# Moving the splits, rotations and tables of a hybrid encoder block from GpSimd to VectorE

## The chip, the cores and the metric

The kernel runs on one core of a Trainium2 chip. A core has a matrix engine (TensorE, PE in the profile), a vector engine (VectorE, DVE), an engine for activation functions (ScalarE, ACT), a general-purpose engine (GpSimd, POOL) and a queue engine that issues the transfers (SyncE, SP). Each engine works through its own list of instructions in order and waits on semaphores for the others. The metric is the device time of one execution in microseconds (us); the time before is the median of three runs.

## The reference

One encoder block on a sequence of 1024 tokens of width 1024, all in float32:

```python
h = _rms_norm(x, norm_mix_g)
proj = h @ w_in            # gla q,k,v,r | gate codes fwd,bwd | swa q,k,v | gates a,b
y_gla = _gla_branch(...) @ w_o_gla     # 4 heads, chunked gated linear attention, both directions
y_swa = _swa_branch(...) @ w_o_swa     # 8 query heads on 2 key heads, window +-128, rotary, sinks
merged = sigmoid(gate_a) * y_gla + sigmoid(gate_b) * y_swa
x = x + merged @ w_out
h2 = _rms_norm(x, norm_ffn_g)
gu = h2 @ w_ffn_in
x = x + (silu(gu[..., :D_FF]) * gu[..., D_FF:]) @ w_ffn_out
```

In the window branch, queries and keys are normalised per head, multiplied by a gain and rotated by position (`x1*cos - x2*sin`, `x2*cos + x1*sin` on the two halves of 64).

## The kernel before, in words

**Products in three parts.** Matrix products run on float32r operands. To keep float32 accuracy each operand is split in two: a rounded high part `h` (a copy by ScalarE) and a low part `l = raw - h` (a subtraction). A product is then the sum of three matmuls, `h*h`, `h*l` and `l*h`. So every weight tile that is loaded gives one ScalarE copy and one subtraction, and so does every operand that the kernel makes itself. `wunit` (lines 62 to 69) does this for a weight tile of 128x512: transfer into `wr` (4 buffers), copy into `wh` (5 buffers), subtraction into `wl` (5 buffers). The subtraction (L68) is made by GpSimd, unless the caller gives another engine: `out_proj(1)` and the first feed-forward products `p11` and `p21` give VectorE.

**Stages in order of time.**

- Start, to about 50 us: the input is loaded in 16 tiles; `x_tile` makes `xh` (ScalarE, L263), `xl` (VectorE, L264) and the sums of squares (`acc`, L270). PE multiplies the first two weight columns as tiles arrive.
- Gated linear attention (GLA), to about 475 us: PE's order is written by hand. The work of 4 heads x 8 chunks goes through stages `g_gates`, `g_sums`, `g_scores`, `g_out`, `g_back_out` and `g_turn`, one slot apart, and between any two of them PE is given a number of dense matmuls of the input projection (`fill`, `slot`; 31 a slot in the middle). `next_unit` keeps the weight tiles of the dense work two units ahead of their use (`AHEAD = 2`). `g_sums` makes from the gates the scaled queries `q2` and keys `kh`, `kl` of a chunk (L360 to L368); `g_scores` splits the values `vh`, `vl` (L378, L379), transposes the keys and computes the scores (`sp`, split into `sh` and `sl` at L395 and L396); `g_out` uses them. GpSimd makes the low parts at L366, L368 and L379.
- Windowed attention, to about 775 us, filled in the same way with dense matmuls: GpSimd makes three of the four tables `qA`, `qB` (cosine and sine times the query gain, L513 to L516). `k_prep` loads the keys and values of a block, splits the values (`vSl`, L557) and normalises and rotates the keys (`norm_rope`, L523 to L543; two of its products on GpSimd at L537 and L538). `k_turn` transposes the rotated keys (L563). `a_prep` normalises and rotates the queries (two products on GpSimd, L577 and L579, the others on VectorE, L581 and L582), then `a_turn`, `a_scores`, `a_probs` and `a_out` follow, each a slot later.
- Branch products, to about 1050 us: `prep_a`, `prep_b` load and split the outputs of the two mixers; `branch_a`, `branch_b` and `out_proj` multiply them by three weight matrices in `hgroup`, two `wunit` tiles for each output tile.
- Feed-forward, the rest: sums and differences of weights on GpSimd and VectorE (`comb`, L848), splits in `wsplit` (VectorE, L830), gates on GpSimd (L878, L921, L937).

**The order.** PE's instructions run in the order of the program. For the other engines a planner puts the instructions in order when the kernel is built, by their place in the program and by when they could start in its own estimate. On the chip each engine keeps that order, so an instruction that waits holds up those behind it on its engine. All transfers are issued by SyncE.

Of the kernel before, what the change touches and what calls it, by code (L numbers as in the profile page):

```python
# [8 lines left out]
F32 = mybir.dt.float32  # L9
# [20 lines left out]
def body(tc, i, out):  # L30
    nc = tc.nc
    with ExitStack() as root:
# [26 lines left out]
            nc.sync.dma_start(out=t, in_=src)  # L59
            return t  # L60

        def wunit(src, n=512, e=None):
            raw = wp.tile([P, n], F32, tag="wr", name=nm("wr"), bufs=4)
            nc.sync.dma_start(out=raw, in_=src)
            h = wp.tile([P, n], FR, tag="wh", name=nm("wh"), bufs=5)
            nc.scalar.activation(h, raw, AF.Copy)  # L66
            l = wp.tile([P, n], FR, tag="wl", name=nm("wl"), bufs=5)
            (e or nc.gpsimd).tensor_tensor(l, raw, h.bitcast(F32), op=ALU.subtract)  # L68
            return h, l

        def mm(o, a, b, start, stop):
# [273 lines left out]
        def g_sums(hd, c):  # L345

            a = gla[hd, c]
            bp = chtile((P, 2, 256))
            for d in range(2):
                mm(bp[:, d], a.lh[:, d], U, True, False)  # L350
                mm(bp[:, d], a.ll[:, d], U, False, True)

            a.sm = gtile("sm", (P, 2, 2), bufs=32)
            nc.vector.tensor_copy(a.sm, bp[:, :, 127:129])
            bc = bp.rearrange("p a (c t) -> p (a c) t", c=2)[:, 0:4:3]
            eb = gtile("eb", (P, 2, P), bufs=1)
            a.en = gtile("en", (P, 2, P))
            nc.scalar.activation(eb, bc, AF.Exp)
            nc.scalar.activation(a.en, bc, AF.Exp, scale=-1.0)
            nc.vector.tensor_tensor(eb, eb, a.qk[:, 0:1].to_broadcast([P, 2, P]), op=ALU.mult)  # L360
            nc.vector.tensor_tensor(a.en, a.en, a.qk[:, 1:2].to_broadcast([P, 2, P]), op=ALU.mult)
            a.q2 = gtile(f"q2{c}", (P, 2, 2, P), FR, bufs=2 if c < 5 else 1)
            a.kh = gtile("kh", (P, 2, P), FR)
            a.kl = gtile("kl", (P, 2, P), FR)
            nc.scalar.activation(a.q2[:, :, 0], eb, AF.Copy)
            nc.gpsimd.tensor_tensor(a.q2[:, :, 1], eb, a.q2[:, :, 0].bitcast(F32), op=ALU.subtract)  # L366
            nc.scalar.activation(a.kh, a.en, AF.Copy)
            nc.gpsimd.tensor_tensor(a.kl, a.en, a.kh.bitcast(F32), op=ALU.subtract)  # L368

        def g_scores(hd, c):  # L370

            a = gla[hd, c]
            need((f"v{hd // 2}", c))
            vr = gtile("vr", bufs=1)
            nc.sync.dma_start(out=vr, in_=scr[f"v{hd // 2}", c][:, (hd % 2) * 256:(hd % 2) * 256 + 256])
            a.vh = gtile("vh", dt=FR)
            a.vl = gtile("vl", dt=FR)
            nc.scalar.activation(a.vh, vr, AF.Copy)  # L378
            nc.gpsimd.tensor_tensor(a.vl, vr, a.vh.bitcast(F32), op=ALU.subtract)  # L379
            kt = chtile((P, 2, P))  # L380
            for d in range(2):
                nc.tensor.transpose(kt[:, d], a.en[:, d], ident)
            a.kth = gtile("kth", (P, 2, P), FR)
            a.ktl = gtile("ktl", (P, 2, P), FR)
            nc.scalar.activation(a.kth, kt, AF.Copy)
            nc.vector.tensor_tensor(a.ktl, kt, a.kth.bitcast(F32), op=ALU.subtract)
            sc = chtile((P, 2, P))
            for d in range(2):
                mm3(sc[:, d], a.kh[:, d], a.kl[:, d], a.q2[:, d, 0], a.q2[:, d, 1], True, True)
            sp = gtile("sp", (P, P))  # L390
            nc.scalar.copy(sp, sc[:, 0])
            nc.vector.copy_predicated(sp, tri, sc[:, 1])
            a.sh = gtile("sh", (P, P), FR)
            a.sl = gtile("sl", (P, P), FR)
            nc.vector.tensor_copy(a.sh, sp)  # L395
            nc.vector.tensor_tensor(a.sl, sp, a.sh.bitcast(F32), op=ALU.subtract)  # L396
# [113 lines left out]
        qA = sc_.tile([P, KT, P], F32, tag="qA", name="qA")  # L510
        qB = sc_.tile([P, KT, P], F32, tag="qB", name="qB")
        gb_ = [qg[:, None, h * 64:(h + 1) * 64].to_broadcast([P, KT, 64]) for h in range(2)]
        nc.gpsimd.tensor_tensor(qA[:, :, 0:64], cosb, gb_[0], op=ALU.mult)  # L513
        nc.gpsimd.tensor_tensor(qA[:, :, 64:128], cosb, gb_[1], op=ALU.mult)
        nc.vector.scalar_tensor_tensor(qB[:, :, 0:64], sinb, -1.0, gb_[1], op0=ALU.mult, op1=ALU.mult)
        nc.gpsimd.tensor_tensor(qB[:, :, 64:128], sinb, gb_[0], op=ALU.mult)  # L516

        def inv_norm(raw, n, sq, scale, epsv, eps_t):
            ss = sw.tile([P, n], F32, tag=f"ss{n}", name=nm("ss"))
# [6 lines left out]
        def norm_rope(raw, n, t, gain, scale, epsv, eps_t):  # L526

            sq = sw.tile([P, n, P], F32, tag=f"sq{n}", name=nm("sq"))
            rs = inv_norm(raw, n, sq, scale, epsv, eps_t)
            qn = sw.tile([P, n, P], F32, tag=f"qn{n}", name=nm("qn"))  # L530
            for h in range(n):
                nc.vector.scalar_tensor_tensor(qn[:, h], raw[:, h], rs[:, h:h + 1], gain,
                                               op0=ALU.mult, op1=ALU.mult)
            c = cosb[:, t:t + 1].to_broadcast([P, n, 64])
            s = sinb[:, t:t + 1].to_broadcast([P, n, 64])
            b = sq
            nc.gpsimd.tensor_tensor(b[:, :, 0:64], qn[:, :, 64:128], s, op=ALU.mult)  # L537
            nc.gpsimd.tensor_tensor(b[:, :, 64:128], qn[:, :, 0:64], s, op=ALU.mult)  # L538
            nc.vector.tensor_tensor(qn[:, :, 0:64], qn[:, :, 0:64], c, op=ALU.mult)
            nc.vector.tensor_tensor(qn[:, :, 64:128], qn[:, :, 64:128], c, op=ALU.mult)  # L540
            nc.vector.tensor_tensor(qn[:, :, 0:64], qn[:, :, 0:64], b[:, :, 0:64], op=ALU.subtract)
            nc.vector.tensor_tensor(qn[:, :, 64:128], qn[:, :, 64:128], b[:, :, 64:128], op=ALU.add)
            return qn  # L543
# [7 lines left out]
        def k_prep(t):  # L551
            kv = sw.tile([P, 4, P], F32, tag="kvr", name=nm("kvr"), bufs=1)
            need(("skv", t))
            nc.sync.dma_start(out=kv.rearrange("p a b -> p (a b)"), in_=scr["skv", t])
            v2 = kv[:, 2:4].rearrange("p a b -> p (a b)")
            nc.scalar.activation(vSh[t], v2, AF.Copy)
            nc.gpsimd.tensor_tensor(vSl[t], v2, vSh[t].bitcast(F32), op=ALU.subtract)  # L557
            keys[t] = norm_rope(kv[:, 0:2], 2, t, kg, 1.0 / 128, EPS, epst)

        def k_turn(t):  # L560
# [7 lines left out]
        def a_prep(g, n):  # L568
            a = att[g, n] = Chunk()
            need((f"sq{g}", n))  # L570
            qr = sw.tile([P, 4, P], F32, tag="qr", name=nm("qr"))
            nc.sync.dma_start(out=qr.rearrange("p a b -> p (a b)"), in_=scr[f"sq{g}", n])

            b = sw.tile([P, 4, P], F32, tag="sq4", name=nm("sq"))
            a.rs = inv_norm(qr, 4, b, 1.0, EPS * 128, eps128)
            a.qn = sw.tile([P, 4, P], F32, tag="qn4", name=nm("qn"))
            nc.gpsimd.tensor_tensor(b[:, :, 0:64], qr[:, :, 64:128], qB[:, n:n + 1, 0:64].to_broadcast([P, 4, 64]),  # L577
                                    op=ALU.mult)
            nc.gpsimd.tensor_tensor(b[:, :, 64:128], qr[:, :, 0:64], qB[:, n:n + 1, 64:128].to_broadcast([P, 4, 64]),  # L579
                                    op=ALU.mult)  # L580
            nc.vector.tensor_tensor(a.qn, qr, qA[:, n:n + 1].to_broadcast([P, 4, P]), op=ALU.mult)  # L581
            nc.vector.tensor_tensor(a.qn, a.qn, b, op=ALU.add)  # L582
# [133 lines left out]
        def btile(tag, dt=F32, bufs=None):  # L716
            return bt.tile([P, HT], dt, tag=tag, name=nm(tag), bufs=bufs)

        def hgroup(w, u0, ah, al, e=None):
            b = mmtile()  # L720
            for u in range(2):
                h, l = wunit(w[u0, u], e=e)
                for kk in range(4):
                    k = u * 4 + kk
                    c = slice(kk * P, (kk + 1) * P)
                    mm3(b, h[:, c], l[:, c], ah[k], al[k], k == 0, k == KT - 1)
            return b
# [58 lines left out]
        def out_proj(s):  # L786
            a = acc[:, s * HT:(s + 1) * HT]
            for j, m in enumerate((0, 4, 1, 5, 2, 6, 3, 7)):
                xr = fi.tile([P, HT], F32, tag="lx", name=nm("lx"), bufs=2)
                nc.sync.dma_start(out=xr, in_=i["xT"][m, s])  # L790
                y = hgroup(i["w_out"], m, mh, ml, nc.vector if s else None)
                nc.vector.tensor_tensor(xr, y, xr, op=ALU.add)
                d = scratch(f"x1_{m}_{s}")
                nc.sync.dma_start(out=d, in_=xr)
# [97 lines left out]
        def p11(f):  # L892
            F = feats[f]
            F.Y = mmtile()
            if f < NB:
                w = wunit(i["w_fi"][f, 0], e=nc.vector)
            else:
                F.r11 = rload(f, 11)
                w = wsplit(F.r11, 512)
# [3 lines left out]

        def p21(f):
            F = feats[f]
            w = wunit(i["w_fi"][f, 1], e=nc.vector) if f < NB else wsplit(F.r12, 512)
            product(F.Y, w, YX["21"], 4, False, True)
            F.g0 = gate0(F.Y, "a" if f < NA else "g0")

# [264 lines left out]
```

## Time and profile before

| | before |
|---|---|
| median of 3 runs (lowest to highest) | 1748.46 us (1748.05 to 1749.23) |
| profiled execution, its own time | 1748.99 us |
| its span, first to last instruction | 1747.2 us |
| TensorE (PE) busy | 1701.6 us, 97% |
| VectorE (DVE) busy, instructions | 1105.4 us, 63%, 1998 |
| ScalarE (ACT) busy | 866.4 us, 50% |
| GpSimd (POOL) busy, instructions | 564.4 us, 32%, 491 |
| mean granted clock of TensorE | 0.993 |

Busy means that an instruction of the engine is in progress; a matmul's end is modelled, and a few records can be missing. In lists of instructions a line gives the start, the length, the engine, the source line, the operation, output and inputs by the program's names, their sizes, and in square brackets how long the engine had idled before it and what ended that. In groups, the count is followed by busy time, mean length in ns, and the idle time before its members. A waiting row says who waited, for whom, for how long in total, how often, and the longest.

### The profile page before, as it was taken

How to read it: one execution, taken by the hardware profiler on the slowest of the kernel's cores; microseconds unless marked ns; L12 is line 12 of the kernel's file. 1: busy time of each engine (PE TensorE's matmuls, PEld its weight loads, DVE VectorE, ACT ScalarE, POOL GpSimd, SP SyncE). 2: the span in 40 equal slices, each digit the busy share in tenths (PEclk: the TensorE clock that was granted, in tenths of full speed). 3: DMA queues.
4: the chain of work that ended last, by engine and by line, in shares of the span. 5: the costliest groups of instructions: out<-in, count | busy, mean ns of one | idle time of the engine just before them, and what ended most of it. 6: DMA issues, size and time to landing. Idle time of an engine off the chain costs nothing. (4 is left out here: it accounts for less than half of the span.)

```text
span 1747.2 us, 24463 instructions
## 1 busy us (share of the span) xinstructions
PE 1701.6 (97%) x8008; PEld 1408.8 (81%) x8008; DVE 1105.4 (63%) x1998; ACT 866.4 (50%) x2019; POOL 564.4 (32%) x491
## 2 busy tenths in 40 slices
PE   8999999999999999999999999999999999899998
PEld 6788888888778888878878888788888888787776
DVE  6446666664387655536463268877788888789454
ACT  6455766776447656544454456533333333343342
POOL 3444535544353222112455430333343333100000
PEclk9999999999999999999999999999999999999999
DMA  5433343444533232227766645333234434685333
GB/s 193 138 113 103 119 129 120 122 129 138 167 118 118 88 97 91 79 73 246 238 192 187 193 132 181 109 132 127 91 102 146 152 138 140 233 295 170 96 96 103
DMA packets 158496, 246.03 MB, mean 141 GB/s; under 512 B 18111, under 2 KB 47807, under 8 KB 158369
## 3 DMA queue, kind: packets, MB, share of 16 engines
q1 hardware_dynamic: 158368, 244.48, 43.8%
q8 instruction: 63, 1.03, 0.3%
q14 instruction: 65, 0.52, 0.1%
HBM read 177.30 MB, written 67.11 MB: 140 GB/s over the span
## 5 line engine op out<-in xcount | busy, mean ns | idle before, releaser
L68 POOL TENSOR_TENSOR wl<-wr,wh 128x512 fp32r<-128x512 f32 (+1 forms) x226 | 300.3, 1334 | 471.3 <-ACT wh L66 395.3
L66 ACT ACTIVATE wh<-wr 128x512 fp32r<-128x512 f32 (+1 forms) x256 | 158.1, 625 | 133.7 <-PE mm L72 89.6
L72 PE MATMUL mm<-xh,wh 128*128 128x512 f32 x512 | 205.4, 401 | 6.7 <-ACT xh L263 6.7
L72 PE MATMUL mm<-xl,wh 128*128 128x512 f32 x512 | 205.1, 401 | 0.9 <-DVE xl L264 0.9
L72 PE MATMUL mm<-xh,wl 128*128 128x512 f32 x512 | 172.2, 401 | 0.0
L848 POOL TENSOR_TENSOR ws<-wr,wr 128x512 f32<-128x512 f32 x44 | 67.0, 1525 | 231.3 <-DMA wr<-in_w_fi_dram 126.3
L72 PE MATMUL mm<-wh,xh 128*128 128x512 f32 x320 | 127.0, 397 | 2.6 <-ACT st L210 1.3
L72 PE MATMUL mm<-wh,xl 128*128 128x512 f32 x320 | 126.8, 396 | 0.0
L72 PE MATMUL mm<-wl,xh 128*128 128x512 f32 x320 | 126.3, 395 | 0.0
L72 PEld LDWEIGHTS mm<-xh,wh 128*128 128x128 f32 x512 | 98.0, 191 | 23.3 <-ACT xh L263 6.7
L72 PEld LDWEIGHTS mm<-xl,wh 128*128 128x128 f32 x512 | 97.9, 191 | 18.7 <-DVE xl L264 1.9
L72 PEld LDWEIGHTS mm<-xh,wl 128*128 128x128 f32 x512 | 96.0, 191 | 16.7
L829 ACT ACTIVATE wh<-ws 128x512 fp32r<-128x512 f32 x88 | 55.4, 629 | 98.7 <-PE ch L856 41.5
L829 ACT ACTIVATE wh<-a 128x512 fp32r<-128x512 f32 x66 | 41.7, 632 | 103.2 <-PE mm L992 58.0
L830 DVE TENSOR_TENSOR wl<-ws,wh 128x512 fp32r<-128x512 f32 x88 | 76.4, 875 | 13.5 <-ACT wh L829 13.5
L992 PE MATMUL mm<-hl,wh 128*128 128x512 f32 x176 | 70.7, 402 | 11.0 <-DVE hl L967 11.0
L830 DVE TENSOR_TENSOR wl<-a,wh 128x512 fp32r<-128x512 f32 x66 | 45.5, 691 | 55.1 <-ACT wh L829 55.0
L829 ACT ACTIVATE wh<-wr 128x512 fp32r<-128x512 f32 x52 | 32.9, 632 | 77.9 <-PE ch L856 39.3
L72 PEld LDWEIGHTS mm<-wh,xh 128*128 128x128 f32 x320 | 60.3, 188 | 13.9 <-ACT st L210 2.0
L992 PE MATMUL mm<-hh,wh 128*128 128x512 f32 x176 | 70.0, 398 | 1.2 <-ACT hh L966 1.2
L992 PE MATMUL mm<-hh,wl 128*128 128x512 f32 x176 | 70.1, 398 | 0.0
L72 PEld LDWEIGHTS mm<-wh,xl 128*128 128x128 f32 x320 | 60.3, 188 | 10.0
(502 smaller groups left out, 4785.9 us busy)
## 6 DMA issues: line engine op xcount, KB each, us to landing
wr<-in_w_fi_dram SPq DMA_DIRECT2D x102, 256.0 KB, 2.8
wr<-in_w_t_dram SPq DMA_DIRECT2D x80, 256.0 KB, 2.7
wr<-in_w_f_dram SPq DMA_DIRECT2D x64, 256.0 KB, 2.8
B<-c SPq DMA_DIRECT2D x44, 256.0 KB, 2.1
T<-tx SPq DMA_DIRECT2D x44, 256.0 KB, 2.2
a<-in_w_fo_dram SPq DMA_DIRECT2D x44, 256.0 KB, 4.9
hr<-T SPq DMA_DIRECT2D x44, 256.0 KB, 2.7
hr<-B SPq DMA_DIRECT2D x33, 256.0 KB, 4.0
```

The lines of the kernel that those rows point to most:

```text
L66: nc.scalar.activation(h, raw, AF.Copy)
L68: (e or nc.gpsimd).tensor_tensor(l, raw, h.bitcast(F32), op=ALU.subtract)
L72: nc.tensor.matmul(o, a, b, start=start, stop=stop)
L829: nc.scalar.activation(h, src, AF.Copy)
L830: nc.vector.tensor_tensor(l, src, h.bitcast(F32), op=ALU.subtract)
L848: e.tensor_tensor(t, x, y, op=op)
L992: nc.tensor.matmul(ys[m], a[:, c], b, start=f0, stop=f1, skip_group_check=True)
```

## The change

All of GpSimd's work ahead of the feed-forward part becomes VectorE's. Nothing else differs: the same instructions on the same tiles, in the same places of the program. GpSimd keeps its weight sums and gates of the feed-forward part.

```diff
-        def wunit(src, n=512, e=None):
+        def wunit(src, n=512):
...
-            (e or nc.gpsimd).tensor_tensor(l, raw, h.bitcast(F32), op=ALU.subtract)
+            nc.vector.tensor_tensor(l, raw, h.bitcast(F32), op=ALU.subtract)
...
-            nc.gpsimd.tensor_tensor(a.q2[:, :, 1], eb, a.q2[:, :, 0].bitcast(F32), op=ALU.subtract)
+            nc.vector.tensor_tensor(a.q2[:, :, 1], eb, a.q2[:, :, 0].bitcast(F32), op=ALU.subtract)
...
-            nc.gpsimd.tensor_tensor(a.kl, a.en, a.kh.bitcast(F32), op=ALU.subtract)
+            nc.vector.tensor_tensor(a.kl, a.en, a.kh.bitcast(F32), op=ALU.subtract)
...
-            nc.gpsimd.tensor_tensor(a.vl, vr, a.vh.bitcast(F32), op=ALU.subtract)
+            nc.vector.tensor_tensor(a.vl, vr, a.vh.bitcast(F32), op=ALU.subtract)
...
-        nc.gpsimd.tensor_tensor(qA[:, :, 0:64], cosb, gb_[0], op=ALU.mult)
-        nc.gpsimd.tensor_tensor(qA[:, :, 64:128], cosb, gb_[1], op=ALU.mult)
+        nc.vector.tensor_tensor(qA[:, :, 0:64], cosb, gb_[0], op=ALU.mult)
+        nc.vector.tensor_tensor(qA[:, :, 64:128], cosb, gb_[1], op=ALU.mult)
...
-        nc.gpsimd.tensor_tensor(qB[:, :, 64:128], sinb, gb_[0], op=ALU.mult)
+        nc.vector.tensor_tensor(qB[:, :, 64:128], sinb, gb_[0], op=ALU.mult)
...
-            nc.gpsimd.tensor_tensor(b[:, :, 0:64], qn[:, :, 64:128], s, op=ALU.mult)
-            nc.gpsimd.tensor_tensor(b[:, :, 64:128], qn[:, :, 0:64], s, op=ALU.mult)
+            nc.vector.tensor_tensor(b[:, :, 0:64], qn[:, :, 64:128], s, op=ALU.mult)
+            nc.vector.tensor_tensor(b[:, :, 64:128], qn[:, :, 0:64], s, op=ALU.mult)
...
-            nc.gpsimd.tensor_tensor(vSl[t], v2, vSh[t].bitcast(F32), op=ALU.subtract)
+            nc.vector.tensor_tensor(vSl[t], v2, vSh[t].bitcast(F32), op=ALU.subtract)
...
-            nc.gpsimd.tensor_tensor(b[:, :, 0:64], qr[:, :, 64:128], qB[:, n:n + 1, 0:64].to_broadcast([P, 4, 64]),
+            nc.vector.tensor_tensor(b[:, :, 0:64], qr[:, :, 64:128], qB[:, n:n + 1, 0:64].to_broadcast([P, 4, 64]),
...
-            nc.gpsimd.tensor_tensor(b[:, :, 64:128], qr[:, :, 0:64], qB[:, n:n + 1, 64:128].to_broadcast([P, 4, 64]),
+            nc.vector.tensor_tensor(b[:, :, 64:128], qr[:, :, 0:64], qB[:, n:n + 1, 64:128].to_broadcast([P, 4, 64]),
```

The parameter `e` of `hgroup` and the arguments `e=nc.vector` of `out_proj(1)`, `p11` and `p21` fall away, since VectorE is now the only engine of `wunit`.

More of the change, by code (lines that the diff above doesn't have):

```diff
@@ L717, in btile, with hgroup @@
             return bt.tile([P, HT], dt, tag=tag, name=nm(tag), bufs=bufs)
-        def hgroup(w, u0, ah, al, e=None):
+        def hgroup(w, u0, ah, al):
             b = mmtile()
             for u in range(2):
-                h, l = wunit(w[u0, u], e=e)
+                h, l = wunit(w[u0, u])
                 for kk in range(4):
@@ L790, in out_proj @@
                 nc.sync.dma_start(out=xr, in_=i["xT"][m, s])
-                y = hgroup(i["w_out"], m, mh, ml, nc.vector if s else None)
+                y = hgroup(i["w_out"], m, mh, ml)
                 nc.vector.tensor_tensor(xr, y, xr, op=ALU.add)
@@ L895, in p11 @@
             if f < NB:
-                w = wunit(i["w_fi"][f, 0], e=nc.vector)
+                w = wunit(i["w_fi"][f, 0])
             else:
@@ L905, in p21 @@
             F = feats[f]
-            w = wunit(i["w_fi"][f, 1], e=nc.vector) if f < NB else wsplit(F.r12, 512)
+            w = wunit(i["w_fi"][f, 1]) if f < NB else wsplit(F.r12, 512)
             product(F.Y, w, YX["21"], 4, False, True)
```

## The prediction

> **What bounds the kernel now.** I read the page's busy times first, then the stages, then what TensorE (PE) waits for in each stage, and last the queues around the two longest waits.
>
> ```profile
> PE 1701.6 (97%) x8008; PEld 1408.8 (81%) x8008; DVE 1105.4 (63%) x1998; ACT 866.4 (50%) x2019; POOL 564.4 (32%) x491
> ```
> ```profile
> 0.00:50.00 50.00, 41.77 (x167) 31.00 (x167) 33.57 (x50) 31.18 (x52) 14.44 (x15) 0.97 0.53 174
> 50.00:475.00 425.00, 419.59 (x2280) 357.67 (x2280) 232.83 (x545) 266.29 (x757) 196.87 (x192) 1.00 0.42 126
> 475.00:775.00 300.00, 293.24 (x1438) 243.83 (x1436) 183.85 (x505) 171.90 (x539) 88.60 (x96) 0.99 0.32 101
> 775.00:1050.00 275.00, 273.22 (x1193) 224.05 (x1194) 131.62 (x170) 130.69 (x223) 112.08 (x83) 0.99 0.62 191
> ```
>
> The second view is by stage; its columns are the stretch and its length, then PE, weight loads, DVE (VectorE), ACT (ScalarE) and POOL (GpSimd) busy, then PE's granted clock. PE is the bound: only time in which PE idles or runs at a lower clock can be won. In the four stages that the change touches (start; GLA; windowed attention; branch products, up to about 1050 us) PE idles 50-41.77 = 8.2, then 5.4, 6.8 and 1.8 us. POOL is far from full, so its speed is not what is bought; what counts is which of these idle times a POOL instruction makes. What ended the long ones (us in total, times, longest), for start, GLA, attention and branch in turn:
>
> ```profile
> PE mm L72 <- ACT xh L263: 6.7, 1, 6.7
> PE mm L72 <- DVE xl L264: 0.9, 2, 0.7
> ...
> PE ch L72 <- ACT kb L415: 1.4, 1, 1.4
> PE ch L465 <- ACT ob L459: 1.4, 1, 1.4
> PE mm L72 <- ACT st L210: 1.3, 1, 1.3
> ...
> PE ch L563 <- ACT rl L94: 3.8, 1, 3.8
> ...
> PE ch L637 <- ACT p L626: 2.2, 1, 2.2
> PE mm L72 <- POOL wl L68: 1.0, 2, 0.6
> ```
>
> POOL is named for 1.0 us only. The 6.7 us are the first load and stay. The 3.8 us at L563 are put down to ACT; the rows further down show a slow DVE chain behind ACT's part.
>
> **The change, part by part.** 381 of POOL's 491 instructions go to DVE: 226 weight splits (L68), 96 splits of queries, keys and values in GLA, and in attention 8 value splits, 48 rotation products and 3 tables. Nothing is added, and no transfer is moved. DVE gets their work at its own speed, and loses the time by which POOL was stretching its instructions:
>
> ```profile
> 24.96 0.74 DVE L264 SCALAR_TENSOR_TENSOR xl<-xr,g,xh 128x512 fp32r<-128x512 f32 x1
> 26.23 1.53 DVE L264 SCALAR_TENSOR_TENSOR xl<-xr,g,xh 128x512 fp32r<-128x512 f32 x1
> 27.69 1.50 DVE L270 TENSOR_TENSOR acc<-acc,sq 128x512 f32<-128x512 f32 x1
> 29.11 1.77 DVE L264 SCALAR_TENSOR_TENSOR xl<-xr,g,xh 128x512 fp32r<-128x512 f32 x1
> ...
> 26.20 4.14 POOL L68 TENSOR_TENSOR wl<-wr,wh 128x384 fp32r<-128x384 f32 x3 [6.77 <-ACT wh L66]
> ```
>
> The same instruction takes 0.74 us alone and 1.53 or 1.77 while POOL splits weights (start in us, length in us).
>
> *Start.* While POOL made three splits, three DVE instructions took 1.53+1.50+1.77 = 4.80 us, against 3 x 0.74 = 2.22: 2.6 us lost. Three splits on DVE cost at most 3 x 0.69 = 2.07 (0.69 is the length of a split that DVE makes already, L830 from `a`, quoted below). DVE's queue has no gap there, so the last `xl` comes some 0.5 us earlier, and most of PE's 0.7 us goes. The first two splits fall into the time in which DVE, as PE, waits for the first `xh`. Term: -0.5 (bounds 0 and -0.7).
>
> *GLA.* Two groups of the whole trace (count | busy, mean ns | idle before), and single instructions of one slot and a later one:
>
> ```profile
> L830 DVE TENSOR_TENSOR wl<-a,wh 128x512 fp32r<-128x512 f32 x66 | 45.5, 691 | 55.1 <-ACT wh L829 55.0
> L395 DVE CAST sh<-sp 128x128 fp32r<-128x128 f32 x32 | 17.5, 546 | 1.0
> L361 DVE TENSOR_TENSOR en<-en,qk 128x256 f32<-128x256 f32 x32 | 13.4, 418 | 0.0
> ```
> ```profile
> 204.34 0.74 POOL L368 TENSOR_TENSOR kl<-en,kh 128x256 fp32r<-128x256 f32 x1
> ...
> 207.47 0.27 PE L72 MATMUL ch<-q,kl 128*128 128x128 f32 x1
> ...
> 221.04 0.23 DVE L395 CAST sh<-sp 128x128 fp32r<-128x128 f32 x1
> ```
>
> POOL's 192 instructions here are 96 weight and 96 chunk splits: on DVE 96 x 0.69 + 96 x 0.42 = 106.6 us. Given back: `sh` alone 32 x (0.546-0.23) = 10 us; other stretched groups are not counted. DVE would go from 232.8 to at most 329 us of 425, or 77%: not full. The long waits of PE here end with ACT, so I take no gain (bounds 0 and all idle time, -5.4; what may be lost is under new waits, below). What hides the moved splits is slack: in the slot shown `kl` was ready at 205.08 and PE took it at 207.47, 2.4 us later. On DVE a split is shorter, 0.42 for 0.74, but it queues in order with the chunk's chain, and what comes after it waits behind it.
>
> *Attention, entry.* This is the largest term. PE is to transpose the first rotated keys (L563) and waits:
>
> ```profile
> 477.13 1.29 POOL L513 TENSOR_TENSOR qA<-cosb,qg 128x512 f32<-128x512 f32 x1 [0.69 <-DMA kg<-in_kg_dram]
> ...
> 478.97 1.18 DVE L96 TENSOR_SCALAR rt<-ss 128x2 f32<-128x2 f32 x1
> ...
> 482.85 0.68 DVE L581 TENSOR_TENSOR qn<-qr,qA 128x512 f32<-128x512 f32 x1
> 484.30 1.34 DVE L539 TENSOR_TENSOR qn<-qn,cosb 128x128 f32<-128x128 f32 x1 [0.77 <-POOL sq L538]
> ...
> 487.03 0.81 DVE L542 TENSOR_TENSOR qn<-qn,sq 128x128 f32<-128x128 f32 x1
> ...
> 505.62 0.28 DVE L542 TENSOR_TENSOR qn<-qn,sq 128x128 f32<-128x128 f32 x1
> ```
> ```profile
> 487.94 0.66 PE L563 MATMUL ch<-ident,qn 128*128 128x128 f32 x2 [3.85 <-ACT rl L94]
> 488.25 0.78 PE L72 MATMUL mm<-xh,wl 128*128 128x512 f32 x1
> ...
> 493.47 0.40 PE L72 MATMUL mm<-xh,wh 128*128 128x512 f32 x1
> 493.71 0.39 PE L72 MATMUL mm<-xl,wh 128*128 128x512 f32 x1
> ```
>
> Beside POOL's tables and products an instruction on 128x2 elements takes 1.18 us and one on 128x128 0.81 to 1.34, against 0.28 for L542 later. Without POOL: four table products from 477.1 on (4 x 0.69) end at 479.9; the inverse norm's four tiny instructions, at no more than 0.28, at 481.0; the value split (0.42), two gain products and six rotation steps (8 x 0.28) at 483.7; one weight split makes it 484.4. PE is there at 487.94-3.85 = 484.1. So the keys are ready about as PE arrives. The stall costs more than itself: the 13 matmuls from 488.25 to 493.47 take 5.2 us, and at the spacing after them (0.24) 3.1, so 2.1 us more go at a lower clock. All of it is 3.85+2.1 = 5.95 us. If the first query block's products (four of 0.42 and two of 0.69, some 3 us) stand ahead of the keys, most of the wait stays. I take -5.0, nearer to the whole because the rows give a finish within 0.3 us of PE's arrival (bounds 0 and -5.95).
>
> *Attention, end.* PE waits 2.2 us for probabilities (L626), then runs slowly:
>
> ```profile
> 769.71 1.23 DVE L612 TENSOR_TENSOR mx<-mx,rs 128x4 f32<-128x4 f32 x1
> ...
> 775.45 1.68 PE L637 MATMUL ch<-ident,p 128*128 128x128 f32 x4 [2.21 <-ACT p L626]
> 779.79 0.60 PE L637 MATMUL ch<-ident,p 128*128 128x128 f32 x4
> ```
>
> From 775.45 to 779.79 PE does four transposes (0.60 at the later row's pace) and seven matmuls (7 x 0.24): 4.3 us for 2.3, so 2.0 are lost to the clock. L612, on 128x4 elements, is stretched to 1.23 us by a POOL split; alone it takes no more than the 0.28 above. So the chain to `p` is up to 0.95 us shorter, less 0.69 if that split now stands ahead on DVE. Term: -0.6 (bounds 0 and -4.2, the wait and its slow stretch).
>
> The Trainium skill, "TensorE: Matmul & The Clock Gate", section "Part 1: The HAM clock gate", lets the clock fall only after an idle window of about 3.4 us; by it a wait of 2.2 us costs no more than itself. This trace differs: 2.21 us sufficed at 775, while GLA's waits of 1.4 left its clock at 1.00. By the page the bound of this term would be -2.2, and the sum the same.
>
> *Branch products.* 83 splits go to DVE, 83 x 0.69 = 57 us on top of 131.6 of 275: 69%. PE's 1.0 us for POOL's splits can go. Term: -0.5 (bounds 0 and all idle time, -1.8).
>
> *After 1050 us* no instruction moves; only the order may shift. Term 0, within 1.5 either way.
>
> *New waits.* After 1050 us DVE splits weights already. There PE's waits for DVE and DVE's own waits for ACT's rounding are
>
> ```profile
> PE mm L855 <- DVE u L925: 2.9, 4, 1.6
> PE mm L855 <- DVE c L931: 1.9, 2, 1.0
> ...
> DVE wl L830 <- ACT wh L829: 77.7, 63, 3.5
> ```
>
> 4.8 us of PE's time in the 475 us of the feed-forward input products; at that rate 1000 us would hold some 10. Here the weight units are made two ahead of their use (`AHEAD`) and the slack above covers one such wait, so I take +1 (bounds 0 and +10).
>
> Sum: -0.5 +0 -5.0 -0.6 -0.5 +0 +1 = -5.6. The profiled execution took 1748.99 us (span 1747.2), 0.5 over the median of the runs, 1748.46: 1743.4 against its own time, 1742.9 against the median. I say 1742.9.
>
> **The rivals.** *The entry's wait stays (no change).* DVE is one queue in order. If query products or further weight splits stand ahead of the key rotation, 2 to 3 us of the wait remain, and the clock may still fall as it did after 2.21. For it: L581, a query product, ran at 482.85 ahead of the keys' L539. Against: it ran while DVE had to wait for POOL's L538, and that gap is gone. Then perhaps -1 of the entry is left: -0.5-1-0.6-0.5+1 = -1.6, about 1747.
>
> *Weight splits block the GLA chain (slower).* A split on DVE waits for ACT's rounding, on average 77.7/63 = 1.2 us, up to 3.5, and the chunk's chain stands behind it. The stage's 45 slots of about 9 us have two weight splits each. It decides where the waits in a slot pass the slack of 2.4 us. With 1 us lost in half of the slots it is +22, and in a third +15, less the 5.6: about 1758; from ten such slots on the kernel is slower by over 0.2%. For it: ACT is busy 266 of these 425 us and waits for DVE in turn. Against: 63 such waits after 1050 us go with only 4.8 us of PE waiting in the products that need those splits. The Trainium skill, same page, section "Architectural detail: the array is 16× 32×32, not 1× 128×128", calls DVE a strict first-in-first-out queue; that is this rival's mechanism.
>
> *More is won.* Both slow stretches go whole, and half of GLA's and of the branch's idle time: -0.7-5.95-4.2-2.7-0.9 = -14.5: 1734.
>
> **How the numbers follow.** About 0.2% (3.5 us) is what a measurement of this kernel can tell from no change. Forecast, 1739 to 1746: 0.47, of which 0.03 lies within 0.2%; more is won: 0.1; the wait stays: 0.25; slower: 0.18. Faster 0.54, same 0.28, slower 0.18. The range for 8 in 10 goes from 1736, inside the greater gain, to 1754, inside the slower rival; the forecast's own is 1739 to 1746.
>
> **What the profile would show.** Right: POOL busy only after 1050 us, with the 110 instructions left; `xl` and the tiny instructions at L96 to L99 never over 1 us before that; L563 without its 3.8 us and the clock at 1.00 between 480 and 500; DVE at 70 to 77% in GLA. Wrong: PE waiting at L72 for `wl`, `kl` or `sl` of DVE slot after slot, or at L563 as before with query products ahead of L539.

## The result and the profile after

The changed kernel takes 1735.41 us, median of 4 runs (1735.19 to 1735.91), against 1748.85 us (1748.05 to 1749.83) of the kernel before on the same chip: a ratio of 0.992, interval 0.991 to 0.994, 13.4 us less. The forecast was 1742.9, 5.6 us less than the median it started from, with a range from 1736 to 1754: the sign was right, the size was less than half of what came, and the time lies just below the range. The largest part that is missing comes from a stage that the forecast put at nothing. The rival called "more is won" (1734) comes nearest in time, though not in its parts: it gave GLA 2.7 us and the attention end 4.2, where 4.6 and 2.0 came.

The page's busy times of the changed kernel:

```profile
PE 1695.9 (98%) x8008; PEld 1407.4 (81%) x8008; DVE 1186.1 (68%) x2379; ACT 876.2 (51%) x2019; POOL 154.1 (9%) x110
```

DVE has 381 instructions more and is busy only 1186.1-1105.4 = 80.7 us longer, while POOL is busy 564.4-154.1 = 410 us less. By stage (columns as before: PE, weight loads, DVE, ACT, POOL, granted clock; then the DMA engines' share and GB/s); the last row is the feed-forward input products:

```profile
50.00:475.00 425.00, 423.13 (x2301) 362.19 (x2302) 276.68 (x746) 273.29 (x765) 0.00 (x0) 1.00 0.43 131
475.00:775.00 300.00, 296.90 (x1466) 247.03 (x1466) 190.10 (x593) 175.69 (x538) 0.00 (x0) 1.00 0.31 97
775.00:1050.00 275.00, 275.00 (x1213) 227.38 (x1212) 174.40 (x273) 139.73 (x232) 0.00 (x0) 1.00 0.64 198
1050.00:1525.00 475.00, 465.45 (x2031) 381.40 (x2030) 373.94 (x492) 179.70 (x301) 153.91 (x106) 0.99 0.44 145
```

Of POOL's 110 instructions, four are short fills at the very start, so the feed-forward part has 106. In GLA DVE comes to 276.7 us, not the 329 that was allowed for; in attention to 190.1, for 183.9 before, though 593 instructions instead of 505 fall into that stretch. PE's idle time falls from 5.4 to 1.9 us in GLA and from 1.8 to nothing in the branch products. What PE still waits for before the branch products, from a list over GLA and one over attention:

```profile
PE ch L465 <- ACT ob L459: 1.4, 1, 1.4
PE mm L72 <- DVE st L146: 1.2, 1, 1.2
...
PE ch L637 <- ACT p L626: 2.9, 8, 1.6
```

GLA's waits for `st` of L210, for `st` of L149 and for `kb` are gone, and so is the wait at L563.

To see where time went in each kernel I set the start times of a few PE instructions against those of before: the first transposes of L382 (GLA begins), the last of L465 (GLA ends), the first and the last matmul of L588 (the attention scores), the first of the last four of L637, the first of L855 (feed-forward) and the first of L992 (output). Change of each stage's length in us, from the one profiled execution of each kernel:

| | GLA | entry | attention end | branch | feed-forward |
|---|---|---|---|---|---|
| length before | 393.3 | 36.1 | 24.6 | 306.4 | 427.9 |
| changed kernel | -4.6 | -6.4 | -2.0 | -2.4 | +0.9 |
| changed kernel, again | -4.6 | -6.4 | -0.5 | -2.3 | +0.1 |
| `w_only` | -4.6 | -1.8 | -0.6 | -2.4 | +1.1 |
| `att_only` | -0.2 | -6.3 | -0.1 | +1.2 | -0.8 |
| `tables_only` | +0.1 | -2.3 | -0.4 | +0.7 | -1.2 |
| `rot_only` | +0.1 | -4.6 | -1.4 | 0.0 | -1.9 |
| `ff_dve` | 0.0 | -2.8 | -1.4 | -0.5 | -4.7 |
| `all_dve` | -4.6 | -6.4 | -0.8 | -2.0 | -6.7 |
| `dup_write` | -4.5 | -6.3 | -1.4 | -1.4 | +0.2 |
| `write3` | -4.6 | -6.3 | -1.2 | -0.4 | +2.6 |
| `read_one` | -4.1 | -6.2 | -0.6 | +7.0 | +6.8 |
| `dup_read` | +9.9 | -6.0 | -2.0 | +12.9 | +15.3 |

The start and the output moved by 1 to 2 us from run to run, also where nothing in them differed (the start: -0.4 and -2.5 in two profiles of the changed kernel), and are left out; so is the body of attention between the scores, which moved by at most 0.5 us but for `read_one` (+3.8) and `dup_read` (+4.0). In the two profiles of the changed kernel GLA and the branch products repeat within 0.2 us. In the four kernels that leave the branch splits on GpSimd the branch stage still moved by -0.5 to +1.2 us, so a difference of 1 us there says nothing. Differences of 1 to 2 us at the attention end and of 2 us at the entry can be the clock alone, as the last section shows.

**The chain in GLA.** PE's wait of 1.28 us at 295.84 before, followed back through ACT, DVE and POOL:

```profile
292.25 1.31 POOL L68 TENSOR_TENSOR wl<-wr,wh 128x512 fp32r<-128x512 f32 x1 [1.86 <-ACT rl L94]
...
292.44 1.14 DVE L98 SCALAR_TENSOR_TENSOR rt<-rt,rl 128x2 f32<-128x2 f32 x1
...
293.51 0.75 POOL L379 TENSOR_TENSOR vl<-vr,vh 128x256 fp32r<-128x256 f32 x1
293.62 0.66 DVE L99 SCALAR_TENSOR_TENSOR ors<-rt,rl 128x2 f32<-128x2 f32 x1
294.31 0.91 ACT L459 ACTIVATE ob<-ob,ors 128x256 f32<-128x256 f32 x2 [1.25 <-DVE ors L99]
295.12 0.67 ACT L210 ACTIVATE st<-mm,rstdt 128x512 f32<-128x512 f32 x1
...
295.84 0.50 PE L72 MATMUL mm<-wh,xh 128*128 128x512 f32 x1 [1.28 <-ACT st L210]
```

PE waits for ACT, as the waiting row says; but ACT had itself idled 1.25 us for `ors`, and `ors` was late because two instructions on 128x2 elements took 1.14 and 0.66 us, the first beside a weight split of POOL, the second beside its split of a chunk's values. The same place in the changed kernel:

```profile
289.76 0.69 DVE L68 TENSOR_TENSOR wl<-wr,wh 128x512 fp32r<-128x512 f32 x1
...
290.53 0.71 ACT L210 ACTIVATE st<-mm,rstdt 128x512 f32<-128x512 f32 x1
...
290.77 0.15 DVE L98 SCALAR_TENSOR_TENSOR rt<-rt,rl 128x2 f32<-128x2 f32 x1
290.96 0.16 DVE L99 SCALAR_TENSOR_TENSOR ors<-rt,rl 128x2 f32<-128x2 f32 x1
291.16 0.91 ACT L459 ACTIVATE ob<-ob,ors 128x256 f32<-128x256 f32 x2
```

The split stands in DVE's own queue now, takes 0.69 us, and the pair takes 0.31 instead of 1.80: 1.49 us less, more than PE's wait of 1.28. But a second thing changed at this place. The planner put ACT's queue in another order: `st` (L210), for which PE had waited behind L459, now runs before it and no longer depends on `ors`. By the rows either change would have been enough for this wait, and they don't separate the two.

PE's wait of 1.43 us for `kb` at 382.78 goes back in the same way, from ACT's L415 over L459 to two rows of DVE:

```profile
378.47 1.50 DVE L436 SCALAR_TENSOR_TENSOR tlb<-kb,decb,thb 128x256 fp32r<-128x256 f32 x1
...
381.09 0.44 DVE L99 SCALAR_TENSOR_TENSOR ors<-rt,rl 128x2 f32<-128x2 f32 x1
```

L436 runs beside POOL's weight split at 378.22 and L99 beside POOL's L379; after, they take 0.48 and 0.15. That is 1.3 of the 1.43 us. Here `kb` stands behind L459 on ACT in both kernels, so the lengths are enough for nearly the whole wait, though some neighbours changed places here too.

**The entry.** Some of the rows of the changed kernel's DVE from the norm of the first keys to the rotated keys, and PE's first transpose:

```profile
474.73 0.16 DVE L98 SCALAR_TENSOR_TENSOR rt<-rt,rl 128x2 f32<-128x2 f32 x1
...
475.66 0.69 DVE L581 TENSOR_TENSOR qn<-qr,qA 128x512 f32<-128x512 f32 x1
...
477.27 0.29 DVE L541 TENSOR_TENSOR qn<-qn,sq 128x128 f32<-128x128 f32 x1
...
478.91 0.38 PE L563 MATMUL ch<-ident,qn 128*128 128x128 f32 x2
```

L581, a query product, still stands ahead of the rotation, but the keys are ready at 477.56 and PE takes them at 478.91 without a wait and at full pace.

### The profile page after: what moved, and what is told of

Same layout as the page of the kernel before. It is cut to its first block, busy times and chain, and to the rows that moved or that the text cites. A ratio compares the mean times of both kernels' runs of the same rounds, so it can differ in the third digit from the quotient of the medians.

```text
span 1733.7 us, 24266 instructions
## 1 busy us (share of the span) xinstructions
PE 1695.9 (98%) x8008; PEld 1407.4 (81%) x8008; DVE 1186.1 (68%) x2379; ACT 876.2 (51%) x2019; POOL 154.1 (9%) x110
## 5 line engine op out<-in xcount | busy, mean ns | idle before, releaser
L68 DVE TENSOR_TENSOR wl<-wr,wh 128x512 fp32r<-128x512 f32 (+1 forms) x256 | 175.1, 687 | 78.5 <-ACT wh L66 75.9
L830 DVE TENSOR_TENSOR wl<-ws,wh 128x512 fp32r<-128x512 f32 x88 | 76.5, 877 | 13.5 <-ACT wh L829 13.5
L992 PE MATMUL mm<-hl,wh 128*128 128x512 f32 x176 | 71.3, 405 | 11.6 <-DVE hl L967 11.6
L992 PE MATMUL mm<-hh,wh 128*128 128x512 f32 x176 | 70.3, 399 | 1.6 <-ACT hh L966 1.6
L992 PE MATMUL mm<-hh,wl 128*128 128x512 f32 x176 | 70.5, 400 | 0.0
L72 PEld LDWEIGHTS mm<-wl,xh 128*128 128x128 f32 x320 | 60.3, 188 | 10.1
```

The costliest lines, as they stand in the source:

```text
L68: nc.vector.tensor_tensor(l, raw, h.bitcast(F32), op=ALU.subtract)
L72: nc.tensor.matmul(o, a, b, start=start, stop=stop)
L830: nc.vector.tensor_tensor(l, src, h.bitcast(F32), op=ALU.subtract)
L992: nc.tensor.matmul(ys[m], a[:, c], b, start=f0, stop=f1, skip_group_check=True)
```

## Experiments

The theories. **A**: any GpSimd instruction on tiles lengthens VectorE's instructions beside it; lengthened small ones hold ScalarE, and ScalarE holds PE. **A2**: only a GpSimd instruction that reads does so, and only to VectorE instructions with two inputs in SBUF. **B**: what counted was the length of GpSimd's own instructions and the hand-over to it and back. **C**: what counted is the order in which the planner puts VectorE's queue, and ScalarE's with it, when more work is on it.

**1. GpSimd works again, for nothing (`dup_read`, `dup_write`).** The changed kernel, with an instruction of GpSimd after each weight split whose result nobody uses. VectorE's queue and ScalarE's have the same order in the two.

```diff
 # dup_read
-            nc.vector.tensor_tensor(l, raw, h.bitcast(F32), op=ALU.subtract)
+            nc.vector.tensor_tensor(l, raw, h.bitcast(F32), op=ALU.subtract); nc.gpsimd.tensor_tensor(raw, raw, h.bitcast(F32), op=ALU.subtract)
 # dup_write
-            nc.vector.tensor_tensor(l, raw, h.bitcast(F32), op=ALU.subtract)
+            nc.vector.tensor_tensor(l, raw, h.bitcast(F32), op=ALU.subtract); nc.gpsimd.memset(raw, 0.0)
```

> The changed kernel, and behind each of the 256 weight splits of VectorE (L68) GpSimd subtracts the same two tiles once more into the raw tile, which nobody uses. Only the contention comes back, no result of GpSimd is waited for before 1050 us. Theory A (GpSimd's instructions stretch VectorE's while both run, and the stretched tiny instructions of the norm chains hold up ScalarE and then PE): short VectorE instructions such as L98 and L436 again take over 1 us beside a weight subtraction, 2 to 6 us of PE waits return before 1050 us, 1738 to 1743 us. Theory B (what cost time was GpSimd's own length, 1.3 us for 0.69, and the hand-over to it): no such wait is left, 1735.4 within 1. Theory C (the planner's other order of ScalarE and VectorE removed the waits): the order here is nearly that of the changed kernel, so again 1735.4 within 1.

> As dup_read, with the same order of instructions, but GpSimd fills the raw tile with zeros instead: it writes and reads nothing. Theory A in its plain form (any GpSimd instruction stretches): some 2 to 6 us of waits come back as in dup_read, less by as much as a fill is shorter. Theory A2 (only GpSimd's reading stretches instructions with two inputs in SBUF): L98, L99 and L436 keep their 0.16 and 0.48 us, 1735.4 within 1.5. Theories B and C: 1735.4 within 1. The Trainium skill, SBUF - State Buffer, section Who interferes with whom, says that a two-input VectorE instruction contends with a GpSimd instruction that reads, not with one that only writes; by it A2 holds.

Measured: `dup_read` 1785.0 us (ratio to the kernel before 1.020, 1.019 to 1.022), `dup_write` 1736.4 (0.993, 0.991 to 0.994). Against the changed kernel the reading instruction costs 50 us and the fill nothing that can be measured. PE's waits in GLA of `dup_read`, the longest three:

```profile
PE ch L72 <- ACT kb L415: 3.4, 3, 2.1
PE mm L72 <- ACT st L210: 3.1, 3, 1.6
PE mm L72 <- DVE st L149: 2.1, 1, 2.1
```

These are the waits of the kernel before, by the same names, and more of them. PE and VectorE wait for GpSimd nowhere there, and ScalarE once, for 1.1 us; the transfers that refill the raw tiles do, in both runs (in GLA 199.2 us in `dup_read` and 156.2 in `dup_write`), and what that costs is the question of the next experiment. So neither the hand-over of results (B) nor the order of the queues (C, the same in both) makes the difference of 49 us between the two. A in its broad form falls with the fill. But the size was far off what I had written (a few us): with the splits on DVE and GpSimd reading as well DVE carries both loads, and PE also waits for the splits themselves.

**2. Is it the buffer that is held? (`write3`, `read_one`)** The added subtraction holds the raw tile, and with it the next transfer, for 1.39 us. Three fills hold it for 3 x 0.53 = 1.6 us without reading; a multiplication by 1.0 holds it as long and reads one tile where the subtraction read two.

```diff
 # write3, behind the split of L68
+ nc.gpsimd.memset(raw, 0.0); nc.gpsimd.memset(raw, 0.0); nc.gpsimd.memset(raw, 0.0)
 # read_one, at the same place
+ nc.gpsimd.tensor_scalar(raw, raw, 1.0, None, op0=ALU.mult)
```

> The changed kernel, and after each weight split GpSimd fills the raw tile three times (3 x 0.53 = 1.6 us, longer than the 1.39 us of the added subtraction that cost 50 us), so the raw buffer is held as long. Theory A2 (only GpSimd's reading stretches VectorE): 1734 to 1738, as the changed kernel. Theory A (any GpSimd work on tiles stretches): 1755 or more. Rival H (what the added subtraction cost was the raw buffer held 1.4 us longer, so later transfers): 1770 to 1790.

> The changed kernel, and after each weight split GpSimd multiplies the raw tile by 1.0 in place: one tile read where the added subtraction read two (that one cost 50 us, three fills of the same tile 3 to 5). Theory A2 (reading stretches, as much as is read): about half, 1748 to 1765. Rival R1 (only instructions with two inputs in SBUF, on both engines, stand in each other's way): 1734 to 1741, as with the fills. Rival R2 (any reading shuts VectorE out for the whole instruction): 1775 or more.

Measured: `write3` 1738.65 us (0.995, 0.994 to 0.997), 5 us over the changed kernel measured beside it (1733.71); `read_one` 1755.97 (1.004, 1.003 to 1.006). In the profiles GpSimd is busy nearly as long with the one as with the other (557.8 and 559.1 us), so the same occupation costs 5 us when it only writes and some 20 when it also reads one tile. That the buffer alone was what `dup_read` paid for is thereby refuted. `write3` lies a little above what A2 gave it; `read_one` falls into its range, and outside those of both its rivals. What lengthens can be read from one small instruction. L98 on 128x2 elements in GLA, in the order before, after, `write3`, `read_one`, `dup_read` (count | busy us, mean ns | idle):

```profile
L98 DVE SCALAR_TENSOR_TENSOR rt<-rt,rl 128x2 f32<-128x2 f32 x16 | 6.7, 419 | 0.4
```
```profile
L98 DVE SCALAR_TENSOR_TENSOR rt<-rt,rl 128x2 f32<-128x2 f32 x17 | 2.7, 159 | 0.3
```
```profile
L98 DVE SCALAR_TENSOR_TENSOR rt<-rt,rl 128x2 f32<-128x2 f32 x17 | 2.7, 158 | 0.3
```
```profile
L98 DVE SCALAR_TENSOR_TENSOR rt<-rt,rl 128x2 f32<-128x2 f32 x16 | 3.2, 198 | 0.3
```
```profile
L98 DVE SCALAR_TENSOR_TENSOR rt<-rt,rl 128x2 f32<-128x2 f32 x16 | 4.5, 281 | 0.3
```

Not at all by fills, a little by a reader of one tile, much by a reader of two. The cast `sh` (L395), which has one input, does feel the fills, so A2 is too narrow in its second half. Its rows after and in `write3`:

```profile
L395 DVE CAST sh<-sp 128x128 fp32r<-128x128 f32 x32 | 7.2, 226 | 0.9
```
```profile
L395 DVE CAST sh<-sp 128x128 fp32r<-128x128 f32 x32 | 9.8, 306 | 0.9
```

That, or the buffer, or a third thing may be the 5 us of `write3`: the order. In `dup_read`, `dup_write` and `read_one` VectorE's queue and ScalarE's are the same from end to end, and 31 of VectorE's 2379 instructions stand at another place than in the changed kernel; in `write3` it is 65. The three weren't told apart. The pair in one order that differs in reading is `dup_write` (1736.4) and `read_one` (1755.97). The Trainium skill, "SBUF — State Buffer", section "Who interferes with whom", states just this division: a VectorE instruction with two SBUF inputs contends with a GpSimd instruction that reads, "not with one that only writes it", while it lists casts among those that can contend with GpSimd without that limit. The trace agrees on both (L98 takes 158 ns with the fills against 159 without; the cast 306 against 226).

**3. Which part of the change wins where (`w_only`, `att_only`, `tables_only`, `rot_only`).** Each is the kernel before with one part of the change: the weight splits; the whole attention part; its three tables; its rotation products and value splits.

```diff
 # w_only
-            (e or nc.gpsimd).tensor_tensor(l, raw, h.bitcast(F32), op=ALU.subtract)
+            (e or nc.vector).tensor_tensor(l, raw, h.bitcast(F32), op=ALU.subtract)
 # tables_only (L513, L514, L516); rot_only does the same to L537, L538, L557, L577, L579; att_only does both
-        nc.gpsimd.tensor_tensor(qA[:, :, 0:64], cosb, gb_[0], op=ALU.mult)
+        nc.vector.tensor_tensor(qA[:, :, 0:64], cosb, gb_[0], op=ALU.mult)
```

> The kernel before with only the 226 weight splits on VectorE; chunk splits, tables, rotations and value splits stay on GpSimd. Theory A: the waits that followed a stretch by a weight split go (start 0.7 us, the three of GLA at 259, 296 and 383 us some 4.6 with what goes with them, attention's end 2.6, branch 1.0), the entry's 6 us stay for the larger part, because the tables and rotations are on GpSimd still: 1740 to 1743. Theory B: about the same for start and branch, but nothing in GLA, where PE waited for no split: 1744 to 1746. Theory that the attention part alone made the gain: 1748.

> The kernel before with only attention's tables, rotations and value splits on VectorE. Theories A and B alike: the entry's wait goes, unless the weight split that stays on GpSimd stretches a step of the key chain: -4 to -6.4 us, the rest as before, 1742.5 to 1745. If the weight splits' stretching was what made the entry late: 1747 to 1749. GLA's waits at 296 and 383 us are as before under A and B, and moved only under C.

> The kernel before with the three attention tables (L513, L514, L516) on VectorE, rotations and value splits still on GpSimd. Before, the tables on GpSimd lay beside the key norm's tiny instructions at L96 to L99, and the rotation products L537, L538 beside L581 and L539. Theory A2: the tables own about half of the entry's 6.4 us: 2 to 4 us, 1745 to 1747. Theory B (the rotation's own length and hand-over are what held PE): the tables alone give less than 1 us, 1748.

> The kernel before with the rotation products (L537, L538, L577, L579) and the value splits (L557) on VectorE, the three tables (L513, L514, L516) still on GpSimd; the other half of the attention part, whose tables alone moved the entry (from the end of GLA to the first scores) by 2.3 us of 6.4. If the two parts add, this one moves the entry by 3.5 to 4.5 us, 1743 to 1746 in all. Theory A2 allows more than the rest, since each of the two can take the clock's fall away (up to 5). Theory B (the rotation's own length and hand-over are the whole of it): 6 or more.

Measured: `w_only` 1738.66 us (0.994, 0.993 to 0.995), 1.3 us below the 1740 to 1743 that A gave it; `att_only` 1742.61 (0.996, 0.995 to 0.997); `tables_only` 1746.3 (0.999, 0.998 to 1.000, which doesn't exclude no change); `rot_only` 1743.45 (0.998, 0.996 to 0.999). The table of stages puts them apart: the weight splits own the whole gain in GLA and in the branch products, the attention part nearly the whole gain at the entry (there the weight splits alone take 1.8, so the parts overlap). Since the 96 chunk splits are still on GpSimd in `w_only` and GLA gains its full 4.6 us there, moving them as well brought nothing to it. Of the entry's two parts the rotation has the larger share. How long PE idles there, and its next matmul, in `tables_only` and then in `rot_only`:

```profile
486.51 0.66 PE L563 MATMUL ch<-ident,qn 128*128 128x128 f32 x2 [2.42 <-ACT rl L94]
486.82 0.77 PE L72 MATMUL mm<-xh,wl 128*128 128x512 f32 x1
```
```profile
483.94 0.41 PE L563 MATMUL ch<-ident,qn 128*128 128x128 f32 x2 [1.58 <-issue]
484.10 0.48 PE L72 MATMUL mm<-xh,wl 128*128 128x512 f32 x1
```

The idle time of 3.85 us falls to 2.42 by the one and to 1.58 by the other (where the profile names nobody as waited for): 1.4 and 2.3 us, which together make 3.7. The two parts nearly add, and each is a lengthened stretch of the same DVE chain. B, which gave the tables under 1 us and the rotation 6 or more, isn't the whole of it; the 0.77 us that DVE idled for POOL's L538 before are its share. The rest of `rot_only`'s 4.6 us is the clock, which did not fall in that execution.

**4. The part that the change left out (`ff_dve`, `all_dve`), and the changed kernel again.** GpSimd's 106 feed-forward instructions (weight sums, gates) on VectorE, alone and on top of the change.

```diff
-            (nc.gpsimd if tag == "g0" else nc.vector).tensor_tensor(g0, g0, r0, op=ALU.mult)
+            nc.vector.tensor_tensor(g0, g0, r0, op=ALU.mult)
...
-            s1 = comb(nc.gpsimd, F.r21, F.r22, ALU.add)
+            s1 = comb(nc.vector, F.r21, F.r22, ALU.add)
...
-            nc.gpsimd.tensor_tensor(p5, p5, p1, op=ALU.add)
+            nc.vector.tensor_tensor(p5, p5, p1, op=ALU.add)
...
-            s3 = comb(nc.gpsimd, F.r11, F.r21, ALU.subtract)
+            s3 = comb(nc.vector, F.r11, F.r21, ALU.subtract)
...
-            nc.gpsimd.tensor_tensor(u2, u2, r1, op=ALU.mult)
+            nc.vector.tensor_tensor(u2, u2, r1, op=ALU.mult)
```

> The changed kernel, with GpSimd's remaining 110 instructions (weight sums and gates of the feed-forward part) on VectorE too. Theory A2 (a GpSimd instruction that reads stretches VectorE's): the stage from L855 on gets shorter by its small stalls, 3 to 6 us, 1729 to 1733 us in all, although VectorE gets some 106 x 0.69 = 73 us more work there. Theory B (only GpSimd's own length or hand-over counted, and these gates are not late): no change, 1735. Rival: VectorE, busy 374 of the 475 us of the feed-forward input products, fills up and PE waits at L855: 1740 or more.

> The kernel before with only GpSimd's 110 feed-forward instructions on VectorE (the part that the change left out); GpSimd keeps everything ahead of it. In the kernel with all of it on VectorE the feed-forward products were 6.7 us shorter than before, and VectorE was busy as long as before there, 375 us for 374. If that is this part's own doing, and not a result of what came before: 5.5 to 9 us, 1739 to 1742. If it needs the earlier part (transfers and the order shifted by it): less than 3.

> The changed kernel once more. All theories: 1735.4 within 1 us. Its trace tells how far the stages differ from run to run: I expect GLA, the attention entry and the branch products to repeat within 0.3 us, and the feed-forward part and the output within 1.5 us.

Measured: `all_dve` 1724.67 us (0.987, 0.985 to 0.989); the changed kernel measured beside it 1733.71 (0.992, 0.990 to 0.994), 0.7 us below what all theories gave it; `ff_dve` 1742.73 against 1748.36 (0.997, 0.995 to 0.998). So `all_dve` beats both kernels of the case, the changed one by 9.0 us, which is more than any theory gave it. `ff_dve` comes 0.7 us above the range of the theory that fits it best. The feed-forward stretch of the kernel before and of `all_dve`:

```profile
1050.00:1525.00 475.00, 465.45 (x2030) 381.97 (x2029) 378.42 (x499) 180.93 (x303) 152.43 (x106) 0.99 0.42 140
```
```profile
1050.00:1525.00 475.00, 471.11 (x2063) 388.74 (x2062) 375.25 (x605) 183.31 (x304) 0.00 (x0) 0.99 0.45 152
```

DVE runs 605 instructions instead of 499 in this stretch of time and is busy 3 us less. Where the time came back, in two of its groups, of the changed kernel and then of `all_dve` (feed-forward products alone):

```profile
L830 DVE TENSOR_TENSOR wl<-ws,wh 128x512 fp32r<-128x512 f32 x87 | 75.8, 880 | 13.5 <-ACT wh L829 13.5
...
L848 DVE TENSOR_TENSOR ws<-wr,ws 128x512 f32<-128x512 f32 x22 | 35.3, 1603 | 0.5
```
```profile
L830 DVE TENSOR_TENSOR wl<-ws,wh 128x512 fp32r<-128x512 f32 x88 | 60.3, 685 | 12.5 <-ACT wh L829 12.5
...
L848 DVE TENSOR_TENSOR ws<-wr,ws 128x512 f32<-128x512 f32 x22 | 15.0, 684 | 0.0
```

The sums that ran beside GpSimd's took 1603 ns and take 684 alone. PE's waits at L855 for `u` (3.3 us in the changed kernel) and for `c` (1.5) are in no list of `all_dve`. In `ff_dve` the stage gains 4.7 us by itself, between the two expectations (5.5 or more if the gain is this part's own, under 3 if it needs the earlier one): most of the 6.7 us is its own, and the other 2 stay unexplained. Its entry is 2.8 us shorter too, although nothing in it was edited: the clock did not fall there in that execution.

## Why the prediction was right and wrong

**Start (-0.5).** The wait for `xl` (0.74 us) is gone, as foreseen; the profiles of the changed kernel give -0.4 and -2.5, of which 2.1 is the clock. No more can be said.

**GLA (0; measured -4.6): the step that failed.** It read "The long waits of PE here end with ACT, so I take no gain". The name in a waiting row is only the last link. One step further, what ended ACT's idle time, gives `ors` of DVE, and the lengths before it, 1.14 and 0.66 us on 128x2 elements and 1.50 for L436, give the rest: the stretch that the prediction had shown for the start was at work in GLA's norms too. The two waits bring 1.28 and 1.43 us, and the wait of 0.6 us for `st` of L149 went as well: 3.3 of the 4.6. The weight loads, which wait earlier than the matmuls, idled 2.2, 2.0 and 1.0 us for the same three, 5.2 in all, and none of it is left; the other 1.3 us may lie there but were not followed one by one. The gain lies inside the prediction's own bound for the stage, -5.4.

**DVE's load in GLA (at most 329 us; measured 276.7).** 106.6 us of work came and 43.9 stayed on the engine; only the 10 us of `sh` had been counted as given back. So DVE is busy 65% of GLA, under the 70 to 77% that was named as a sign of being right. `sh` fell from 546 to 226 ns as the step had it.

**Entry (-5.0; measured -6.4).** The mechanism was right: the keys are ready before PE comes, although L581 stayed ahead of the rotation. The wait of 3.85 us went whole, and the slow stretch behind it made 6.4-3.85 = 2.5 us instead of 2.1. These 2.5 are partly luck: in `ff_dve`, where nothing in the entry was edited, no slow stretch followed its wait of 3.38 us. Taking less than the bound for a late query product was the wrong choice, since that product costs 0.69 and no longer finds a gap.

**Attention end (-0.6; measured -2.0 and -0.5).** PE's wait fell from 2.21 to 1.62 us, the 0.6 of the sum. L612 went from 1.23 to 0.15 us. Whether the slow stretch behind the wait goes too differs from one execution to the next.

**Branch products (-0.5; measured -2.4): a term mis-sized.** It was read from PE's list alone. The list of the weight loads in the kernel before shows four waits for the same splits:

```profile
PEld mm L72 <- POOL wl L68: 2.9, 4, 1.0
```

In the changed kernel and in `w_only` this row is gone; in `att_only`, where GpSimd still makes the splits, it stays (3.1 us), and the stage gains nothing (+1.2).

**New waits (+1) and the slower rival.** Before 1050 us nothing new appeared: the one DVE wait that grew is `st` of L146, from 0.7 to 1.2 us. The rival in which splits block GLA's chain is refuted; the reason stands in the group of the moved splits in GLA:

```profile
L68 DVE TENSOR_TENSOR wl<-wr,wh 128x512 fp32r<-128x512 f32 x96 | 66.2, 691 | 38.1 <-ACT wh L66 35.6 <-PE ch L465 0.6 <-PE mm L72 0.4
```

35.6 us of DVE's idle time for 96 splits is 0.4 us each, a third of the 1.2 that the rival took from the feed-forward part, and well under the slack of 2.4.

**After 1050 us (0 within 1.5).** Feed-forward +0.9 and +0.1, output +1.5 in both profiles of the changed kernel, at the bound. In the first profile the +1.5 is a slow stretch of the clock behind a wait of 3.54 us, where the kernel before waited 2.56 without one.

The terms as measured, -0.4-4.6-6.4-0.1 (the body of attention)-2.0-2.4+0.9+1.5, make the 13.5 us by which PE's last matmul begins earlier. Of the 7.8 us that the forecast lacked, GLA is 4.6 and the branch products 1.9.

What stays open: the changed kernel with the old order of ACT's and DVE's queues wasn't run, so the order's own share in the 4.6 us of GLA isn't measured. At the wait for `st` the new order of ACT's queue is a rival that nothing here excludes; at the wait for `kb` the lengths carry 1.3 of 1.43 us. That reading by GpSimd brings such waits back in an unchanged order is shown by `dup_read` and `dup_write`.

## What to carry to other kernels

When a waiting row names an engine, follow that engine's own idle time at least one step further, and look at the length of the instruction it ends with: an instruction on 128x2 elements that takes 1.1 us is the finding, whatever name stands in PE's row. Work on GpSimd that reads SBUF beside a VectorE with two-input instructions is not free: here VectorE could take 106 such instructions and be busy no longer (1182.8 us in `all_dve`, 1186.1 in the changed kernel), so weigh a move by VectorE's lengthened groups and not by the sum of the moved work. Read the waits of weight loads as well as those of matmuls. And before a shorter instruction is given the credit for a wait that went, compare the order of the queues: a planner that gets other lengths and engines may have put the awaited instruction elsewhere.

## What the runs showed of the hardware

**The clock's fall hangs on more than the length of the wait.** The changed kernel in its two executions, at the same place of the program after the same wait (first the one, then the other):

```profile
763.33 1.53 PE L637 MATMUL ch<-ident,p 128*128 128x128 f32 x4 [1.62 <-ACT p L626]
764.62 0.48 PE L72 MATMUL mm<-xh,wh 128*128 128x512 f32 x1
764.93 0.40 PE L72 MATMUL mm<-xl,wh 128*128 128x512 f32 x1
```
```profile
761.17 1.63 PE L637 MATMUL ch<-ident,p 128*128 128x128 f32 x4 [1.62 <-ACT p L626]
762.45 0.78 PE L72 MATMUL mm<-xh,wh 128*128 128x512 f32 x1
763.02 0.63 PE L72 MATMUL mm<-xl,wh 128*128 128x512 f32 x1
```

1.62 us of waiting halved the pace in the second and not in the first, and in `ff_dve` a wait of twice that length did not:

```profile
486.71 0.41 PE L563 MATMUL ch<-ident,qn 128*128 128x128 f32 x2 [3.38 <-ACT rl L94]
486.88 0.48 PE L72 MATMUL mm<-xh,wl 128*128 128x512 f32 x1
```

In the records of the granted clock the half-speed stretches inside a kernel are 3.41 us long, or twice that, and the distances between them are multiples of the same 3.41 us (in the kernel before one begins at 42.4 us and the next at 486.1, 130 times 3.413 later). From that the clock seems to be set once per such window, and a wait to count by how it lies in its window; no run moved a wait on purpose, so this is a reading of the records and not an experiment. The Trainium skill, "TensorE: Matmul & The Clock Gate", section "Part 1: The HAM clock gate", lets the clock fall after an idle window of about 3.4 us. These traces differ, as the prediction's 2.21 us did: here 1.62 us were enough. What follows for measuring: a stage that has a wait of 1.6 to 3.9 us can move by some 2 us between executions of the same code.

**Both engines lengthen.** In the feed-forward part of the changed kernel a sum of GpSimd's takes 1.28 us while VectorE is idle, and a sum of each at the same time 1.65 and 1.78:

```profile
1179.78 1.65 POOL L921 TENSOR_TENSOR p<-p,p 128x512 f32<-128x512 f32 x1 [2.03 <-ACT p L920]
1180.20 1.78 DVE L848 TENSOR_TENSOR ws<-wr,ws 128x512 f32<-128x512 f32 x1
...
1185.49 1.28 POOL L848 TENSOR_TENSOR ws<-wr,wr 128x512 f32<-128x512 f32 x1 [4.06 <-DVE wl L830]
1186.81 0.69 DVE L848 TENSOR_TENSOR ws<-ws,wr 128x512 f32<-128x512 f32 x1 [1.40 <-POOL ws L848]
```

VectorE loses 1.1 us there, more than the 0.69 that it needs to make GpSimd's sum itself. So in `all_dve`, where GpSimd has no share, VectorE runs 106 instructions more than in the changed kernel and is busy 3 us less.
